# A hybrid encoder layer on one core: the memory attention in two lanes, longer steps for the power, and the w_down sums in the places of x

## The chip, the cores and the metric

The kernel runs on one core of a Trainium2 chip. Its time is the time of one execution on the device, in microseconds (us); several executions of the same program give a median and a range. The profile is of one execution. PE is the TensorE matmul, PEld its weight load, DVE the VectorE, ACT the ScalarE, POOL the GpSimd engine and SP the engine whose queue issues every DMA of this kernel.

## The reference

One layer over 2048 tokens of 1024 channels, all in f32. After an RMS norm a large projection feeds three mixers; their outputs are gated, merged and projected back, and an MLP follows.

```
h = rmsnorm(x, g_mix);  z = h @ w_in
q_na = rmsnorm(q_na, g_na_q) * 32**-0.5;  k_na = rmsnorm(k_na, g_na_k)
h_na  = neighbourhood_attention(q_na, k_na, v_na, rpb)     # 8 heads of 32, window 8 x 16 of a 32 x 64 grid
h_m   = mlstm(...) forwards + backwards                    # 4 heads, 64 / 128
q = rmsnorm(q_mem) * 64**-0.5;  k = rmsnorm(k_mem)         # 4 heads of 64
h_mem = softmax(q @ k.T) @ v                               # into 256 memory tokens
y = gate0 * (h_m @ w_proj_mlstm) + gate1 * (h_na @ w_proj_na) + gate2 * (h_mem @ w_proj_mem)
x = x + y @ w_out
x = x + square(relu(rmsnorm(x, g_ffn) @ w_up)) @ w_down
```

## The kernel before

Each f32 product is made of three matmuls on a high and a low part (`mm3`, L232 to L234). Weights come in units of 512 KB: a load (L172), the high part by ACT (L176) and the low part by DVE (L177). The large MLP products are replaced by seven of quarter size instead of eight, for which sums of blocks of w_down are made ahead (`sums_down`).

There are three phases. **Phase 1** takes the tokens in four blocks of 512. In a block come, in this order, the query and key columns of the neighbourhood attention (four groups of 24 matmuls, one for each tile of 128 tokens), the mLSTM's queries and keys with their convolution (`conv`: four groups, whose PSUM result ACT copies out at L654, and some seven DVE operations on each), the neighbourhood values with the memory queries (L519 to L530), the mLSTM's values, in blocks 2 and 3 the 24 groups of the gates (`gate`, copied out at L599), and the output gates. Phase 2 is the scan of the mLSTM with the remaining gates, phase 3 the merge, the output projection and the MLP.

The order of PE's work is the order in which the program is written. After every two steps of a group (six matmuls), now and then four, a **tick** happens: `tick` calls each of three streams once, and a stream gives one piece of small work to the engines. `self.tk` counts the ticks modulo 4.

- `na_qk` (one unit for each tile of tokens): squares by ACT (L917), their sums by DVE (L919), the reciprocal root by POOL with a power (`rstd`, L324 and L325), the product by DVE (L922), PE transposes (L927), high and low parts, stores to DRAM (`s_qs`, `s_ks`). A `yield` ends a piece.
- `mem_unit`, the same for the memory queries, followed by scores (L1184), maximum (L1187), exponential (L1191), transposes (L1204), copies (L1206, tile `mpT`) and the values (L1214).
- `na_stream`, the neighbourhood attention proper. A unit is four heads; queries and keys are loaded by six DMAs (L1008, L1009: `naq`, `nak`), the values by two (`nav`) and a table of biases for each head (`nab`, L1033). A head's scores are L1042, its bias and maximum L1045, its exponential L1047, its scaling L1050, its transposes L1061 five ticks later, and the values L1075. A head starts every four ticks, in block 3 every two.

`unit_stream(q, lanes)` has so many units under way as there are lanes; a lane names the values of `tk` at which its unit may step. Only PE's order is fixed by the program. For ACT, DVE, POOL and SP a scheduler takes operations in the order in which it expects them to be ready, with a priority that the kernel lowers or raises (`cur_priority`), so that an operation can stand on its engine well ahead of work that was written before it. Each of these engines then works strictly in its own order, SP with its waits too.

`sums_down` loads two units of w_down (tiles `dw`, L576), makes four differences in place on DVE at a low priority (L579), and stores both to `s_t` (L101). Eight of these belong to block 2 and eight to block 3, each at every third gate. `x_tile` gives the two buffers (`xt`, 512 KB each) through which tiles of x come in, `x_junk` a tile for squares of which only the sum is used.

## Time and profile before

| what | value |
|---|---|
| median of three runs | 2989.27 us (2983.28 to 2989.3) |
| profiled execution: its time | 2988.64 us |
| profiled execution: span from first to last instruction | 2986.9 us |
| mean granted clock of TensorE | 0.995 |
| PE busy | 2910.6 us (97%) |
| DVE / ACT / POOL busy | 2070.4 / 1195.1 / 237.1 us |
| HBM read / written | 453.63 MB / 176.55 MB |

A row of a list of waits names who waited, for whom, the total, the number of times and the longest. A row of a timeline has the start, the length, the engine, the line and the operation, and in brackets the idle time before it with what ended it. A row of windows has, for a stretch of time, each engine's busy time with its number of instructions, the granted clock, and the DMA's share and rate.

### The profile page before, as it was taken

Reading aid. Unit: us, or ns where it says so; the run is one execution under the profiler, and the core shown is the slowest. Engines: PE = TensorE matmul, PEld = TensorE weight load, DVE = VectorE, ACT = ScalarE, POOL = GpSimd, SP = SyncE. Lnnn points to the kernel's source line nnn. Section 1 sums busy time; section 2 is a strip of 40 time slices with the busy share of each in tenths; the row PEclk is TensorE's granted clock in tenths of the full one; section 3 lists DMA queues with packets and bytes.
Section 4 is the critical chain, followed back from the end, with each engine's and each line's share of the span. In section 5 each row is a group of like instructions: output and inputs, shape, how many; then the busy total and the mean of one; then the engine's idle time right before and its main releaser. Section 6 shows DMA issues by size and latency. Waiting matters only on the chain.

```text
span 2986.9 us, 41900 instructions
## 1 busy us (share of the span) xinstructions
PE 2910.6 (97%) x15028; PEld 2374.8 (80%) x15028; DVE 2070.4 (69%) x3557; ACT 1195.1 (40%) x2198; POOL 237.1 (8%) x389
## 2 busy tenths in 40 slices
PE   8999999999999899999999999999999999999999
PEld 6778788878877677778888888888878888888887
DVE  6676775567654765674769888666676888885666
ACT  6454654344543333342233333543312433344331
POOL 3020210011000322330000000000000000000000
PEclk9999999999999999999999999999999999999999
DMA  8776777867799667789535444766874444466655
GB/s 276 225 253 202 231 227 240 266 217 217 240 283 307 195 199 234 240 276 315 183 110 169 155 152 155 275 191 224 268 235 128 137 155 151 154 226 225 195 182 165
DMA packets 341712, 632.97 MB, mean 212 GB/s; under 512 B 29344, under 2 KB 151008, under 8 KB 341504
## 3 DMA queue, kind: packets, MB, share of 16 engines
q1 hardware_dynamic: 341504, 630.30, 65.4%
q8 instruction: 118, 1.93, 0.3%
q14 instruction: 90, 0.74, 0.1%
HBM read 453.63 MB, written 176.55 MB: 211 GB/s over the span
## 4 chain that ended last, share of the span: by engine, by line
PE 55%; DVE 2%; DMA 2%; issue 1%; ACT 0%; POOL 0%; SPq 0%; DVEq 0%; ACTq 0%; POOLq 0%
PE mm L232 18%; PE mm L234 18%; PE mm L233 18%; PE mm L1339 0%; DVE h L900 0%; DMA og<-s_o 0%; DMA wr<-in_w_units_dram 0%; DMA hf<-s_hf 0%; DVE ev L1495 0%; ACT hf L896 0%; POOL rs L325 0%; DVE acc L1488 0%; DVE ws L177 0%; DVE h L888 0%; DMA X<-s_a 0%
## 5 line engine op out<-in xcount | busy, mean ns | idle before, releaser
L232 PE MATMUL mm<-X,ws 128*128 128x512 f32 x1152 | 448.5, 389 | 0.0
L234 PE MATMUL mm<-X,ws 128*128 128x512 f32 x1152 | 448.2, 389 | 0.0
L233 PE MATMUL mm<-X,ws 128*128 128x512 f32 x1152 | 448.1, 389 | 0.0
L232 PE MATMUL mm<-hT,ws 128*128 128x512 f32 x896 | 375.6, 419 | 12.1 <-ACT cz L654 5.5
L177 DVE TENSOR_TENSOR ws<-wr,ws 128x1024 fp32r<-128x1024 f32 (+1 forms) x212 | 263.0, 1246 | 142.8 <-ACT ws L176 137.7
L234 PE MATMUL mm<-hT,ws 128*128 128x512 f32 x896 | 353.6, 395 | 0.0
L233 PE MATMUL mm<-hT,ws 128*128 128x512 f32 x896 | 353.4, 394 | 0.0
L233 PE MATMUL mm<-X 128*128 128x512 f32 x896 | 348.8, 389 | 2.5 <-DVE X L1462 2.5
L234 PE MATMUL mm<-X 128*128 128x512 f32 x896 | 348.7, 389 | 0.5 <-DVE X L1462 0.5
L232 PE MATMUL mm<-X 128*128 128x512 f32 x896 | 348.7, 389 | 0.4 <-ACT X L1461 0.4
L1461 ACT ACTIVATE X<-X 128x1024 fp32r<-128x1024 f32 x176 | 187.0, 1063 | 319.4 <-DMA X<-s_t 124.5
L1462 DVE TENSOR_TENSOR X<-X 128x1024 fp32r<-128x1024 f32 x176 | 214.3, 1224 | 132.8 <-ACT X L1461 132.0
L176 ACT ACTIVATE ws<-wr 128x1024 fp32r<-128x1024 f32 (+1 forms) x212 | 223.5, 1059 | 164.7 <-PE mm L234 91.8
L232 PE MATMUL mm<-ws,hT 128*128 128x512 f32 (+2 forms) x704 | 260.9, 371 | 9.3 <-ACT cz L654 5.1
L234 PEld LDWEIGHTS mm<-X,ws 128*128 128x128 f32 x1152 | 216.2, 188 | 45.1
L233 PEld LDWEIGHTS mm<-X,ws 128*128 128x128 f32 x1152 | 216.2, 188 | 44.9
L232 PEld LDWEIGHTS mm<-X,ws 128*128 128x128 f32 x1152 | 216.2, 188 | 44.5
L234 PE MATMUL mm<-ws,hT 128*128 128x512 f32 (+2 forms) x704 | 249.8, 355 | 1.1 <-DVE hT L434 1.1
L233 PE MATMUL mm<-ws,hT 128*128 128x512 f32 (+2 forms) x704 | 249.0, 354 | 0.3 <-DVE ws L177 0.3
L202 ACT ACTIVATE ws<-wr 128x512 fp32r<-128x512 f32 x224 | 135.3, 630 | 219.9 <-PE mm L234 139.3
L232 PEld LDWEIGHTS mm<-hT,ws 128*128 128x128 f32 x896 | 170.2, 190 | 54.1 <-issue 9.8
L234 PEld LDWEIGHTS mm<-hT,ws 128*128 128x128 f32 x896 | 169.6, 189 | 39.0
(266 smaller groups left out, 4855.3 us busy)
## 6 DMA issues: line engine op xcount, KB each, us to landing
wr<-in_w_units_dram SPq DMA_DIRECT2D x308, 512.0 KB
s_s<-u SPq DMA_DIRECT2D x32, 1024.0 KB
X<-s_s SPq DMA_DIRECT2D x64, 512.0 KB
X<-s_t SPq DMA_DIRECT2D x64, 512.0 KB
s_g<-ev SPq DMA_DIRECT2D x96, 256.0 KB
ev<-s_g SPq DMA_DIRECT2D x96, 256.0 KB
s_a<-u SPq DMA_DIRECT2D x96, 256.0 KB
X<-s_a SPq DMA_DIRECT2D x48, 512.0 KB
```

The source lines that it names most:

```text
L176: nc.scalar.activation(w[:, 0], raw, AF.Copy)
L177: nc.vector.tensor_tensor(w[:, 1], raw, w[:, 0].bitcast(F32), ALU.subtract)
L202: nc.scalar.activation(hi, src, AF.Copy)
L232: mm(out, lhs[0], rhs[0], start=first, stop=False)
L233: mm(out, lhs[0], rhs[1], start=False, stop=False)
L234: mm(out, lhs[1], rhs[0], start=False, stop=last)
L1461: nc.scalar.activation(hi, src, AF.Copy)
L1462: nc.vector.tensor_tensor(lo, src, hi.bitcast(F32), ALU.subtract)
```

## The change

Memory attention gets two lanes, each of which steps every four ticks, in place of one that steps every two; one `yield` fewer stands before the scores and one fewer before the transposes. The tiles `mq`, `me` and `mpT` are doubled. The queries and keys of the neighbourhood attention step every two ticks instead of every four, with five pauses instead of two: from the sums to the product were four ticks, now there are six; from the product to the transposes there are four as before. `zna` has four buffers instead of three. `sums_down` uses the two buffers of x and is split: the loads are given at one gate, the differences and stores at the next, so that the eight sums of a block take its first sixteen gates. The biases have three buffers instead of four, and a unit of the neighbourhood attention that starts while no other is under way waits eight ticks after its loads instead of four. The squares for a norm are written over their input.

```diff
-NAB = 4
+NAB = 3
...
-        self.prep(xt, gbc, xt, self.x_junk())
+        self.prep(xt, gbc, xt, self.t("ev", [128, D], EV[1], BF16))
...
-        self.streams = [self.unit_stream(self.qkq, [(1,)]), self.unit_stream(self.memq, [(0, 2)]), self.na_stream()]
+        self.streams = [self.unit_stream(self.qkq, [(1, 3)]), self.unit_stream(self.memq, [(0,), (2,)]), self.na_stream()]
...
-            z = self.t("zna", [128, 512], 3)
+            z = self.t("zna", [128, 512], 4)
...
         if b in GATES_1:
+            sums = None
             for j in range(24):
                 if j == 22 and b + 1 < NB:
                     self.prep_x()
                 self.gate(b, j)
-                if j % 3 == 0:
-                    self.sums_down(8 * GATES_1.index(b) + j // 3)
+                if j < 16:
+                    sums = sums or self.sums_down(8 * GATES_1.index(b) + j // 2)
+                    sums = next(sums, None) and sums
...
+        r = [self.x_tile(self.a["w_units"][self.down[half * FF // 256 + q][0]]) for half in range(2)]
+        yield True
         prio = self.tc.cur_priority
         self.tc.cur_priority = prio + LOW
-        r = [self.t("dw", [128, 1024], 2) for _ in range(2)]
-        for half in range(2):
-            nc.sync.dma_start(r[half], self.a["w_units"][self.down[half * FF // 256 + q][0]])
...
         r = self.rstd(ss, 32, "q")
         yield
+        yield
+        yield
         nc.vector.tensor_tensor(z, z, r.unsqueeze(2).to_broadcast([128, 16, 32]), ALU.mult)
+        yield
         yield
...
-                last = self.na_unit(*todo.pop(0), last)
+                last = self.na_unit(*todo.pop(0), last, 4 if cur else 8)
...
-        q = self.t("mq", [128, 2, 2, 128], 1, F32R)
+        q = self.t("mq", [128, 2, 2, 128], 2, F32R)
         self.mem_trans(z, q, self.gmqk[:, 0:1])
-        yield
         yield
...
-            e = self.t("me", [128, 2, 256], 2)
+            e = self.t("me", [128, 2, 256], 4)
...
         yield
         yield
-        yield
         ptp = []
...
-            pT = self.t("mpT", [128, 4, 128], 2)
+            pT = self.t("mpT", [128, 4, 128], 4)
```

The same instructions are issued as before, apart from their tiles' names; in phases 2 and 3 they stand on every engine in the same order. In phase 1 they move. Three places of it follow; line numbers are those of each kernel (a memory exponential is L1191 before and L1190 now, a reduction of `na_qk` L919 and L916, its product L922 and L921, a copy out of the convolution L654 and L651, a load through `x_tile` L461).

ACT, ahead of the first convolution group of block 1. Before:

```order
L944 ACTIVATE stk_312_2122<-tr_310_2110,gna_404 128x2x128
L1047 ACTIVATE nsb_319_2153,sm_321_2156<-nsb_319_2153,sm_320_2154 128x440
L1191 ACTIVATE me_337_2223,sm_336_2222<-mx_333_2206,sm_335_2220 128x256 x2
L176 ACTIVATE ws_324_2165<-wr_324_2164 128x2x528
L1047 ACTIVATE nsb_344_2246,sm_346_2249<-nsb_344_2246,sm_345_2247 128x440
L1191 ACTIVATE me_341_2232,sm_340_2231<-mx_334_2207,sm_339_2229 128x256 x2
L654 ACTIVATE cz_348_2255<-mm_325_2169 128x512
```

And with the change:

```order
L1047 ACTIVATE nsb_320_2172,sm_322_2175<-nsb_320_2172,sm_321_2173 128x320
L1064 ACTIVATE npt_330_2203<-tr_329_2199 120x384
L944 ACTIVATE stk_314_2143<-tr_312_2131,gna_404 128x2x128
L1215 ACTIVATE mho_333_2231<-mx_332_2222 128x256
L651 ACTIVATE cz_339_2252<-mm_326_2188 128x512
```

The exponentials of block 0's last memory unit stood between the queries and keys and the copy `cz`; now that unit's last operation (`mho`) comes before it.

DVE, the sums of squares of block 1's last tile of tokens and the product that needs POOL's power. Before:

```order
L919 TENSOR_REDUCE sm_395_2514<-sq_394_2512 128x16
L1050 TENSOR_SCALAR nsb_319_2153<-nsb_319_2153,sm_322_2158 128x320
L922 TENSOR_TENSOR zna_323_2162<-zna_323_2162,rs_396_2516 128x512
L1187 TENSOR_REDUCE sm_335_2220<-mx_333_2206 128x2
L1045 ISA nsb_344_2246,sm_345_2247<-mx_343_2244,nab0_1_0_3_1948 128x320
```

And with the change:

```order
L916 TENSOR_REDUCE sm_395_2610<-sq_394_2608 128x16
L945 SCALAR_TENSOR_TENSOR stk_314_2143<-tr_312_2131,gna_404,stk_314_2143 128x2x128
L1050 TENSOR_SCALAR nsb_320_2172<-nsb_320_2172,sm_323_2177 128x320
L921 TENSOR_TENSOR zna_324_2181<-zna_324_2181,rs_396_2612 128x512
L1216 TENSOR_TENSOR mho_333_2231<-mx_332_2222,mho_333_2231 128x256
L1045 ISA nsb_335_2243,sm_336_2244<-mx_334_2241,nab0_1_0_2_2034 128x320
```

One operation stood between sums and product, now two; the memory maximum (L1187) behind the product is gone from there.

SP's queue in block 3, from a bias of the unit of rows 6 to the loads of the unit of rows 7. Before:

```order
L1033 DMA nab6_1_1_3_9628<-in_rpb_dram 128x440
L1008 DMA naq7_0_9653<-s_qs_96 32x4x256
L1009 DMA nak7_0_9654<-s_ks_97 32x4x512
L101 DMA s_t5_191<-dw_1686_9479 128x2x512
L101 DMA s_t5_191<-dw_1687_9480 128x2x512
L1008 DMA naq7_0_9653<-s_qs_96 32x4x256
L1009 DMA nak7_0_9654<-s_ks_97 32x4x512
L1008 DMA naq7_0_9653<-s_qs_96 32x4x256
L1009 DMA nak7_0_9654<-s_ks_97 32x4x512
```

And with the change:

```order
L101 DMA s_t6_192<-xt_1648_9365 128x2x512
L101 DMA s_t6_192<-xt_1649_9367 128x2x512
L101 DMA s_hna_131<-nho_1552_8912 256x1x256
L461 DMA xt_1685_9543<-in_w_units_dram 128x1024
L461 DMA xt_1686_9545<-in_w_units_dram 128x1024
L101 DMA s_g3_95<-ev_1704_9637 128x512
L172 DMA wr_1705_9646<-in_w_units_dram 128x1024
L1033 DMA nab6_1_1_2_9665<-in_rpb_dram 128x440
L1008 DMA naq7_0_9690<-s_qs_96 32x4x256
L1009 DMA nak7_0_9691<-s_ks_97 32x4x512
L1008 DMA naq7_0_9690<-s_qs_96 32x4x256
L1009 DMA nak7_0_9691<-s_ks_97 32x4x512
```

The stores of a sum no longer divide the loads of queries and keys. The loads of the next sum (`xt`) now stand one DMA behind the stores of the last, in the same two buffers.

More of the change, by code (lines that the diff above doesn't have):

```diff
@@ L442, in rms_x @@
             xt = self.x_tile(self.a["x"][r0:r0 + 128])
-            nc.scalar.activation(self.x_junk(), xt, AF.Square, accum_out=ss[:, t:t + 1])
+            nc.scalar.activation(xt, xt, AF.Square, accum_out=ss[:, t:t + 1])
             yield
@@ L448, in rms_x @@
         self.rb = self.gbc[:, b % 2 * TB:(b % 2 + 1) * TB]
-        dg = self.t("zna", [128, 512], 3).rearrange("p (t c) -> p t c", t=4)
+        dg = self.t("zna", [128, 512], 4).rearrange("p (t c) -> p t c", t=4)
         nc.vector.tensor_tensor(dg, self.ident.unsqueeze(1).to_broadcast([128, 4, 128]),
@@ L462, in x_tile @@
         return xt
-    def x_junk(self):
-        self.n += 1
-        return self.p_x.tile([128, D], BF16, name=f"xq_{self.n}", tag="xq", bufs=1)
     def lhs_tok(self, hT, k, t):
@@ L1010, in na_load_qk, with na_unit @@
         return q, k
-    def na_unit(self, g, hg, half, before):
+    def na_unit(self, g, hg, half, before, wait):
         nc = self.nc
@@ L1016, in na_unit @@
         nr = 8 if g in (0, 7) else 11
-        u = dict(g=g, hg=hg, half=half, nk=nr * 40, pts=[], h=0, wait=4)
+        u = dict(g=g, hg=hg, half=half, nk=nr * 40, pts=[], h=0, wait=wait)
         u["qk"] = before["qk"] if half else self.na_load_qk(g, hg, kr0, nr)
@@ L1134, in mem_rms @@
         for t in range(2):
-            nc.scalar.activation(self.x_junk(), mt[:, t], AF.Square, accum_out=ss[:, t:t + 1])
+            nc.scalar.activation(mt[:, t], mt[:, t], AF.Square, accum_out=ss[:, t:t + 1])
         rm = self.rstd(ss, D, "m")
```

## The prediction

> **What bounds the kernel now.** I read the page's first part, then windows by phase, then PE's waits in phase 1, and last the timelines round the largest of them.
>
> ```profile
> span 2986.9 us, 41900 instructions
> PE 2910.6 (97%) x15028; PEld 2374.8 (80%) x15028; DVE 2070.4 (69%) x3557; ACT 1195.1 (40%) x2198; POOL 237.1 (8%) x389
> ```
>
> ```profile
> 0.00:969.00 969.00, 924.18 (x5803) 758.79 (x5803) 615.54 (x1390) 484.61 (x1016) 109.37 (x217) 0.99 0.78 245
> 969.00:1376.00 407.00, 385.19 (x2112) 292.67 (x2113) 266.73 (x524) 154.62 (x412) 127.69 (x172) 0.98 0.73 231
> 1376.00:2986.90 1610.90, 1601.24 (x7116) 1323.29 (x7114) 1188.13 (x1643) 555.85 (x771) 0.00 (x0) 1.00 0.56 187
> ```
>
> PE is the bound (first number after each stretch's length). The change takes no matmul away, and phases 2 and 3 keep their order on every engine, so what it can win lies in the first row: 969.00 less 924.18 is 44.8 us of PE idle, and what the clock lost behind it. PE's waits in that stretch:
>
> ```profile
> PE mm L232 <- ACT cz L654: 10.6, 5, 2.7
> PE mx L232 <- ACT ws L176: 7.5, 1, 7.5
> PE mx L1042 <- DMA nav<-s_vna: 5.4, 1, 5.4
> PE tr L1061 <- DVE nsb L1050: 4.7, 2, 2.6
> PE mm L232 <- ACT zif L528: 4.2, 4, 1.7
> PE mm L232 <- DMA hT<-s_hT: 4.0, 1, 4.0
> PE mx L1214 <- ACT mpT L1206: 2.1, 2, 1.3
> ```
>
> The 7.5 us are the first weights at the start and the 4.0 us the reload of hT at the end of the phase; the change touches neither. The other five rows make 27.0 us in 14 pieces. Some are followed by a stretch of lower clock (the number before the last two):
>
> ```profile
> 81.00:85.00 4.00, 4.00 (x16) 2.96 (x15) 3.90 (x5) 0.84 (x2) 0.00 (x0) 0.57 0.94 272
> ...
> 231.00:235.00 4.00, 4.00 (x16) 2.97 (x16) 3.55 (x9) 0.18 (x1) 0.00 (x0) 0.57 0.76 208
> ...
> 644.00:648.00 4.00, 3.94 (x13) 3.33 (x14) 2.41 (x8) 1.69 (x5) 0.13 (x1) 0.57 0.81 164
> ...
> 869.00:873.00 4.00, 3.80 (x12) 3.14 (x12) 1.05 (x4) 0.66 (x2) 0.00 (x0) 0.50 1.06 408
> ```
>
> That is 4.00 times 0.43, 1.7 us, at each of the first three and 2.0 us at the last: 7.1 us. The pool is 27.0 + 7.1 = 34.1 us, 1.1% of the time. The sum is made against the profiled execution's own 2988.64 us (0.6 below the median of the three runs).
>
> The Trainium skill, "TensorE: Matmul & The Clock Gate", section "What's actually happening", has the clock fall after an idle window of about 3.4 us. By that rule the first three stretches, each behind idle pieces below 2.8 us, would not exist and no clock would come back with them; the trace shows them, so the measurement decides.
>
> **The change part by part.** First the w_down sums. In block 3 SP's queue, and PE, read:
>
> ```profile
> 853.23 0.68 SPq L1009 DMA_DIRECT2D nak<-s_ks  x1
> 860.67 0.90 SPq L101 DMA_DIRECT2D s_t<-dw  x2
> 861.62 0.87 SPq L1008 DMA_DIRECT2D naq<-s_qs  x1
> ...
> 864.29 0.47 SPq L1009 DMA_DIRECT2D nak<-s_ks  x1
> ```
>
> ```profile
> 863.22 0.40 PE L233 MATMUL mm<-hT,ws 128*128 128x512 f32 x1
> 863.45 0.40 PE L234 MATMUL mm<-hT,ws 128*128 128x512 f32 x1
> 869.20 0.60 PE L1042 MATMUL mx<-nak,naq 96*128 96x320 f32 x1 [5.35 <-DMA nav<-s_vna]
> ```
>
> SP stood from 853.9 to 860.7 for the differences of a sum, with four of the six loads of the next unit behind it; PE waited 5.35 us and lost 2.0 us of clock. At the end of block 2 the same happened to a tile of x:
>
> ```profile
> 603.11 0.91 SPq L172 DMA_DIRECT2D wr<-in_w_units_dram  x2
> 615.93 2.19 SPq L101 DMA_DIRECT2D s_t<-dw  x2
> ```
>
> ```profile
> 637.86 0.65 PE L1061 MATMUL tr<-ident,nsb 128*120 128x128 f32 x4 [2.09 <-DVE nsb L1050]
> ...
> 644.05 0.81 PE L1061 MATMUL tr<-ident,nsb 128*120 128x128 f32 x4 [2.57 <-DVE nsb L1050]
> ```
>
> The late tile kept DVE behind until the first of these two waits, 2.09 us. Sums cost 5.35 + 2.0 + 2.09 = 9.4 us now. With the change all eight are done by the sixteenth gate, far from the tile of x, and the order shows queries and keys in one piece. But sixteen pairs of stores remain in the same queue, each waiting for low-priority work of DVE. Bounds: nothing to 9.4 us back; I take two thirds, **-6.3**.
>
> Next the time for the powers. Block 1, DVE, then ACT, then PE:
>
> ```profile
> 203.58 0.69 DVE L922 TENSOR_TENSOR zna<-zna,rs 128x512 f32<-128x512 f32 x1 [3.08 <-POOL rs L325]
> 204.19 0.69 DVE L1187 TENSOR_REDUCE sm<-mx 128x2 f32<-128x512 f32 x1
> ```
>
> ```profile
> 204.91 0.48 ACT L1191 ACTIVATE me<-mx,sm 128x256 f32<-128x256 f32 x1 [6.15 <-DVE sm L1187]
> ...
> 208.25 0.59 ACT L654 ACTIVATE cz<-mm 128x512 f32<-128x512 f32 x1
> ```
>
> ```profile
> 208.90 0.50 PE L232 MATMUL mm<-hT,ws 128*128 128x512 f32 x1 [2.50 <-ACT cz L654]
> ```
>
> ```profile
> 359.55 0.50 PE L232 MATMUL mm<-hT,ws 128*128 128x512 f32 x1 [1.63 <-ACT cz L654]
> ```
>
> DVE stands for POOL's power; the memory maximum is queued behind, ACT waits for that maximum, and the convolution's copy is queued behind ACT's exponentials. The longer steps hardly move this: pauses hold PE's transposes back, but the scheduler still puts the product two or three DVE operations behind the sums, as the order shows. So I keep the total of
>
> ```profile
> DVE zna L922 <- POOL rs L325: 42.4, 15, 3.3
> ...
> DVE nsb L1045 <- DMA nab<-in_rpb_dram: 5.8, 4, 1.8
> ```
>
> as it is. What does go is what stood behind: two lanes finish the last memory unit before the next block's convolution, so no maximum and no exponential lies between power and copy. The 2.50 and 1.63 us come back whole. The 2.57 us at 644 sit behind a power too, and no memory work was in it; with its clock it is 4.3 us, half of which I take for the shifted steps. Together -4.1 - 2.1 = **-6.2** (bounds 0 and 8.4).
>
> The fourth convolution group of block 1 is late because DVE is full; block 0's also:
>
> ```profile
> 230.59 0.39 PE L232 MATMUL mm<-ws,hT 128*128 128x272 f32 x1 [2.72 <-ACT cz L654]
> ```
>
> With the clock this is 4.4 us. A memory unit's maxima, scaling and output (three rows of a list by line) leave this stretch:
>
> ```profile
> L1194 DVE TENSOR_TENSOR me<-me,sm 128x512 f32<-128x512 f32 x32 | 21.9, 685 | 0.1
> L1187 DVE TENSOR_REDUCE sm<-mx 128x2 f32<-128x512 f32 x32 | 21.7, 678 | 0.1
> ...
> L1218 DVE TENSOR_TENSOR mho<-mx,mho 128x256 fp32r<-128x256 f32 x16 | 6.7, 421 | 14.3 <-ACT mho L1217 14.2
> ```
>
> Twice 685, twice 678 and 421 ns are 3.1 us of DVE, about the wait; as some of it falls ahead of the wait's cause I take half, **-2.2** (0 to 4.4). Block 0's two convolution waits (10.6 less 2.50, 1.63 and 2.72: 3.8, with clock 5.5) have no earlier memory unit to lose; the third tile's q/k work comes later, for which a quarter, **-1.4** (0 to 5.5).
>
> The values of a memory unit came two ticks behind the last transposes, now four: the 2.1 us for mpT go, **-2.1** (0 to 2.1). The zif waits (4.2 us, a copy behind DVE's backlog) ease a little: **-1.0** (0 to 4.2). Doubled tiles and squares written in place cost nothing: the operations are the same, and ACT has half its time free behind PE.
>
> Against it: a bias is asked for two ticks after its buffer's scores, so three buffers leave four ticks of lead at rate two where four left six. From the rows at 863 a matmul starts every 0.23 us; six make a tick of 1.4 us, so 5.6 us of lead instead of 8.4. DVE waited 5.8 us for biases in all; I let it wait that once more and PE pay it: **+5.8**. Its bounds are 0 and the 32 us of the slow case below. The eight ticks at a block's start delay the end of the stream by four ticks, 5.6 us; in the built order its last values still stand ahead of the last output gates on PE, so that no tick runs empty at the end.
>
> Sum: -6.3 - 6.2 - 2.2 - 1.4 - 2.1 - 1.0 + 5.8 = -13.4; 2988.64 - 13.4 = **2975.2 us**.
>
> **Rivals.** (B) The change doesn't do what it says: powers and convolution stall as before, only elsewhere. For it: the 42.4 us above and the order. Left are sums, mpT and biases: -6.3 - 2.1 + 5.8 = -2.6, 2986.0 us. (C) Every piece of the pool goes and the biases cost their 5.8: -28.3, 2960.3 us. For it: all pieces are short queues behind one another, which one loosening can end together; against it: the powers stay. (D) Slower, by SP's queue. The loads of a sum now wait for the last sum's stores to land, since they use the same two buffers. A transfer of 512 KB took
>
> ```profile
> 1241.81 3.62 DMA wr<-in_w_units_dram
> ```
>
> in the chain of waits, so SP stands some 3.6 us, with biases and weights behind, sixteen times. In block 3, where heads come every two ticks, a bias can then come after the 5.6 us of lead, DVE stands, and the transposes of that head are late as at 637 and 644: 4.7 / 2 = 2.3 us and 1.7 us of clock for each of eight sums, 32 us; -19.2 + 32 = +12.8, 3001.4 us. It decides from 19.2 / 8 = 2.4 us a sum. Against it: a store held SP for up to 12 us before (603 to 616) and only two pieces reached PE.
>
> The Trainium skill, "DMA: Bandwidth & Descriptors", section "Anatomy of one DMA", speaks against the change here: a wait is held by the issuing queue, and completion of a write to HBM takes about 2 us beside the bytes. An estimate by its fit is 2.0 + 1.2 = 3.2 us for a store of 512 KB, near the 3.62 us of the row; no row shows such a store's own landing.
>
> **How the numbers follow.** Forecast (A) 0.52, B 0.25, C 0.11, D 0.12. About 0.2%, 6 us, is what a measurement of this kernel can tell from no change. Below 2983.3 us lie nearly all of A (0.48), C (0.11) and a fifth of B (0.05): faster 0.64. Within: the rest of A (0.04), most of B (0.19) and an edge of D (0.02): 0.25. Slower: D and a little of B, 0.11. The range runs from C's value to just over B's, 2961 to 2988; some 0.05 lie below and 0.13 above.
>
> **What would show it.** In PE's waits of phase 1: cz at about 5 us (right), at 10 (B) or gone (C); the 5.4 us for a unit's loads gone, with SP's wait for s_t spread over more and shorter pieces; mpT gone; the L922 wait still near 42 us (if it is below 25, my reading of the steps was wrong and C is nearer). DVE's wait for biases above 12 us, or new waits of L1061 in block 3, speak for D. Phases 2 and 3 must last as long as before to within 3 us; if they differ by more, the sum was made over the wrong stretch.

## The result

The changed kernel takes **3005.66 us** (median of four runs, 3004.55 to 3008.78), the kernel before beside it 2989.28: a ratio of **1.0064, 95% interval 1.005 to 1.0078**. It is slower by 16.4 us in the medians and by some 19 by the ratio; 2975.2 us was forecast, in a range of 2961 to 2988. The profiled execution has a span of 3003.5 us (2986.9 before) and a mean granted clock of 0.989 (0.995).

PE's waits up to phase 2, answering to the list that the prediction shows:

```profile
PE tr L1061 <- DVE nsb L1050: 13.9, 4, 7.7
PE mx L1042 <- DMA nab<-in_rpb_dram: 13.2, 2, 6.6
PE mx L1042 <- DMA s_g<-ev: 8.4, 1, 8.4
PE mx L232 <- ACT ws L176: 7.2, 1, 7.2
PE mm L232 <- DMA hT<-s_hT: 4.0, 1, 4.0
PE mm L232 <- ACT cz L651: 3.9, 2, 3.5
PE mm L232 <- ACT zif L524: 1.1, 2, 0.6
```

What was to go went: the convolution's copy from 10.6 to 3.9 us, zif from 4.2 to 1.1, mpT altogether. But before the transposes of a head (L1061) and the first scores of an attention unit (L1042) PE now waits 35.5 us (13.9 + 13.2 + 8.4) instead of 10.1.

Where they lie shows when phase 1 is cut at the copies of the gates on ACT (L599 before, L596 after): up to block 2's first gate, its 24 gates, the way to block 3's first gate, its 24 gates, to phase 2's first gate, the rest. The second number of a row is the length, the third PE's busy time, the number before the last two the clock, the next the DMA's share. Before:

```profile
0.00:444.60 444.60, 418.31 (x2595) 346.62 (x2596) 308.13 (x700) 244.92 (x515) 79.82 (x114) 0.99 0.75 235
444.60:602.10 157.50, 157.50 (x961) 127.93 (x960) 80.98 (x169) 67.36 (x137) 3.21 (x23) 1.00 0.83 257
602.10:759.90 157.80, 149.97 (x957) 124.51 (x959) 110.47 (x250) 78.52 (x167) 20.85 (x40) 0.99 0.69 214
759.90:943.20 183.30, 176.66 (x1202) 142.01 (x1202) 108.79 (x265) 86.00 (x188) 5.48 (x40) 0.98 0.88 278
982.40:2986.90 2004.50, 1973.04 (x9183) 1605.51 (x9181) 1442.32 (x2144) 708.39 (x1179) 118.75 (x154) 1.00 0.60 196
```

After:

```profile
0.00:427.70 427.70, 413.41 (x2598) 346.33 (x2599) 303.64 (x679) 246.06 (x514) 76.11 (x113) 1.00 0.75 238
427.70:583.30 155.60, 155.60 (x927) 126.20 (x929) 85.92 (x181) 65.93 (x133) 3.18 (x23) 1.00 0.85 274
583.30:752.40 169.10, 154.30 (x998) 129.48 (x991) 109.15 (x251) 81.69 (x172) 21.28 (x39) 0.96 0.65 199
752.40:957.30 204.90, 181.06 (x1179) 144.16 (x1181) 114.49 (x276) 85.08 (x189) 5.85 (x42) 0.93 0.84 259
997.50:3003.50 2006.00, 1974.73 (x9182) 1607.81 (x9180) 1443.87 (x2144) 708.13 (x1179) 118.99 (x154) 1.00 0.60 196
```

The changed kernel is 16.9 us ahead at block 2's first gate and 18.8 at its last. It loses 11.3 us on the way to block 3 and 21.6 us in block 3's gates; with +1.0 to phase 2 and +1.5 behind, the difference of the spans, 16.6 us, is complete. In block 3's gates 23.8 us are idle (204.90 less 181.06). PE is also busy there 8.8 us longer than in the same gates of e9 below, where it never waits (172.30): the mean clock of the stage is 0.93 here and 1.00 there.

Two more lists, DVE's waits and SP's, of the changed kernel:

```profile
DVE zna L921 <- POOL rs L325: 40.4, 16, 4.3
DVE nsb L1045 <- DMA nab<-in_rpb_dram: 27.8, 14, 5.9
```

```profile
SPq L461 <- DMA s_t<-xt: 43.6, 21, 4.9
```

The wait for POOL's power is what it was (42.4), that for biases five times as long (5.8), and SP stands 43.6 us for the landing of the sums' stores. One piece of block 3, SP's queue, then PE:

```profile
814.02 1.03 SPq L101 DMA_DIRECT2D s_t<-xt  x2
815.15 1.16 SPq L1033 DMA_DIRECT2D nab<-in_rpb_dram  x1
819.13 1.62 SPq L461 DMA_DIRECT2D xt<-in_w_units_dram  x2
...
824.29 0.73 SPq L1008 DMA_DIRECT2D naq<-s_qs  x1
...
828.29 0.43 SPq L1009 DMA_DIRECT2D nak<-s_ks  x1
```

```profile
837.47 0.70 PE L1042 MATMUL mx<-nak,naq 96*128 96x440 f32 x1 [6.63 <-DMA nab<-in_rpb_dram]
```

The loads of a sum stand some 4 us behind its predecessor's stores, the unit's queries and keys behind them, and its first scores come 8.7 us after the last of these loads was given. My first theory (**S**) was that SP's wait for the landing makes the unit late. Rivals: **N**, three bias buffers are too few; **L**, the longer steps put the units later; and, from e7 on, **T**, the traffic of sixteen dense gates.

### The profile page after: what moved, and what is told of

Read it like the earlier page. It is cut to its first block, busy times and chain, and to the rows that moved or that the text cites. A ratio compares the mean times of both kernels' runs of the same rounds, so it can differ in the third digit from the quotient of the medians.

```text
span 3003.5 us, 41885 instructions
## 1 busy us (share of the span) xinstructions
PE 2915.3 (97%) x15028; PEld 2383.0 (79%) x15028; DVE 2074.8 (69%) x3557; ACT 1196.9 (40%) x2198; POOL 234.4 (8%) x389
## 2 busy tenths in 40 slices
DMA packets 341712, 632.97 MB, mean 211 GB/s; under 512 B 29344, under 2 KB 151008, under 8 KB 341504
## 4 chain that ended last, share of the span: by engine, by line
PE 55%; DVE 2%; DMA 1%; issue 0%; ACT 0%; SPq 0%; POOL 0%; DVEq 0%; ACTq 0%; POOLq 0%
PE mm L232 18%; PE mm L234 18%; PE mm L233 18%; DMA hf<-s_hf 1%; PE mm L1337 0%; DMA wr<-in_w_units_dram 0%; PE pn L859 0%; DVE h L897 0%; PE pn L862 0%; DVE ev L1493 0%; DVE acc L1486 0%; ACT hf L893 0%; POOL rs L325 0%; DMA X<-s_a 0%; DVE ws L177 0%
## 5 line engine op out<-in xcount | busy, mean ns | idle before, releaser
L176 ACT ACTIVATE ws<-wr 128x1024 fp32r<-128x1024 f32 (+1 forms) x212 | 223.3, 1058 | 158.1 <-PE mm L234 86.6
```

What stands on the lines that cost most here:

```text
L176: nc.scalar.activation(w[:, 0], raw, AF.Copy)
```

## The experiments

All times below are medians; each ratio is against the kernel before on the same chip (2985.2 to 2988.3 us there). The stages are those of the rows above, read from one profiled execution of each. What lies behind them took 2004.1 to 2010.5 us in these executions, though nothing was changed there, so a few us of a single reading can be chance. e1, e2, e9, e10 and e18 leave out the differences of some or all sums: they are probes, not kernels to use.

| kernel | us | ratio, 95% interval | to block 2 | its gates | way to block 3 | its gates | to phase 2 |
|---|---|---|---|---|---|---|---|
| before | 2989.28 | | 444.6 | 157.5 | 157.8 | 183.3 | 39.2 |
| the change | 3005.66 | 1.0064 (1.005, 1.0078) | 427.7 | 155.6 | 169.1 | 204.9 | 40.2 |
| e1 sums copied | 2964.48 | 0.993 (0.9914, 0.9946) | 431.8 | 156.4 | 153.3 | 172.3 | 39.0 |
| e2 before, sums copied | 2970.39 | 0.9952 (0.9935, 0.9968) | 447.7 | 157.5 | 149.0 | 174.3 | 38.2 |
| e3 four biases | 3012.22 | 1.0091 (1.0074, 1.0108) | 429.5 | 158.0 | 171.8 | 202.5 | 39.8 |
| e4 every third gate | 2985.21 | 1.0003 (0.9993, 1.0012) | 429.5 | 156.5 | 169.1 | 183.2 | 40.0 |
| e5 sums back | 2986.18 | 0.9994 (0.9983, 1.0004) | 433.2 | 156.6 | 165.0 | 182.3 | 40.2 |
| e6 sums alone | 3016.34 | 1.0099 (1.0085, 1.0114) | 442.6 | 161.6 | 161.2 | 203.5 | 39.3 |
| e7 GpSimd's queue | 3027.67 | 1.0129 (1.0115, 1.0143) | 454.6 | 165.9 | 182.1 | 176.1 | 39.2 |
| e8 three gates | 2985.90 | 0.9993 (0.9984, 1.0003) | 428.4 | 156.5 | 169.0 | 181.7 | 40.8 |
| e9 copied in block 3 | 2974.23 | 0.9955 (0.9941, 0.9969) | 431.0 | 159.4 | 166.3 | 172.3 | 40.3 |
| e10 copied in block 2 | 2991.11 | 1.0012 (1.0002, 1.0021) | 430.2 | 156.5 | 152.0 | 203.7 | 39.3 |
| e11 blocks 1 and 2 | 3005.43 | 1.0059 (1.0047, 1.0072) | 442.2 | 170.2 | 174.9 | 172.4 | 40.0 |
| e12 spread | 2981.56 | 0.9984 (0.9974, 0.9994) | 428.7 | 156.4 | 152.1 | 189.7 | 47.0 |
| e13 spread, four biases | 2980.56 | 0.9983 (0.9974, 0.9992) | 430.3 | 156.5 | 149.9 | 189.9 | 47.5 |
| e14 spread, old steps | 2988.90 | 1.0 (0.9992, 1.0009) | 430.6 | 156.4 | 153.6 | 192.9 | 48.1 |
| e15 six and ten | 2988.75 | 1.0011 (1.0001, 1.002) | 428.4 | 156.5 | 158.1 | 191.7 | 42.8 |
| e16 seven and nine | 2986.46 | 1.0 (0.9991, 1.001) | 429.0 | 156.7 | 161.3 | 190.6 | 41.3 |
| e17 two pairs | 2992.07 | 1.0018 (1.0009, 1.0027) | 434.6 | 156.5 | 156.3 | 195.3 | 40.2 |
| e18 copied, dense | 2987.18 | 1.0006 (0.9995, 1.0017) | 430.8 | 156.5 | 158.0 | 195.4 | 40.0 |

### What the sums cost, and in whose company

In e1, and likewise in e2 for the sums of the kernel before:

```diff
-                if j < 16:
-                    sums = sums or self.sums_down(8 * GATES_1.index(b) + j // 2)
-                    sums = next(sums, None) and sums
+                if j % 3 == 0:
+                    q = 8 * GATES_1.index(b) + j // 3
+                    for half in range(2):
+                        self.store(self.scr["t"][q // 2][:, half, :, q % 2],
+                                   self.a["w_units"][self.down[half * FF // 256 + q][0]].rearrange("p (n c) -> p n c", n=2))
```

> The changed kernel without its w_down sums: at every third gate the two weight halves are copied from memory to memory into the place of the sums, by transfers that wait for nothing (the differences are left out, so the output is not the reference's). Theory S (SP is held by the sums' loads, which wait until the stores of the sum before have landed in the same two buffers, and the loads of the next attention unit stand behind): the 6.63, 6.61 and 8.37 us ahead of a unit's first scores go, most of the 2.76, 4.35 and 7.69 us at the end of block 2 as well, 37.7 us in all less what stays of them, and the time is 2962 to 2978 us. Theory N (three bias buffers are too few; 14 waits of VectorE for biases, 27.8 us): the waits stay, and the time is above 2995. Theory L (longer steps put the attention units later): also above 2995.

> The kernel before without its sums, copied in the same way at the same gates (differences left out). It prices what the sums cost the kernel before: I put 9.4 us on them, so 2980 us; beside the run of the changed kernel without sums it gives what the other parts of the change are worth where no sum disturbs them: my sum has 13.0 us less 5.8 for the biases.

With copies in place of the sums the changed kernel takes 2964.48 us, in S's range and far from N's and L's. The kernel before takes 2970.39: there the sums cost 14.8 us more than such copies, not my 9.4. So the other parts of the change are worth 5.9 us where no sum disturbs them (the prediction's terms for them: 12.9 less 5.8, 7.1). In the profiled executions they win 15.9 us up to block 2's first gate, and 4.3 of these are lost again on the way to block 3 (153.3 against 149.0).

One thing about these probes matters below. A copy waits for nothing, so the scheduler did not leave it at its gate: the first is given at 89 us, and of the sixteen that e1 writes behind block 3's gates one is given during them. The copies given during these gates (their number, the ns that an issue took, the first and the last time), in e1 and in e18, a later probe with twice as many:

```profile
L101 SPq DMA_DIRECT2D s_t<-in_w_units_dram x1: 598/598/598, 892.4 to 892.4; - x1
```

```profile
L101 SPq DMA_DIRECT2D s_t<-in_w_units_dram x29: 537/594/1162, 748.4 to 883.7; - x29
```

So e1's 172.3 us are block 3's gates all but free of the sums' transfers (e2 gives five copies there, e9 three), not gates with sparse copies.

In e3:

```diff
-NAB = 3
+NAB = 4
...
-            pT = self.t("mpT", [128, 4, 128], 4)
+            pT = self.t("mpT", [128, 4, 128], 3)
```

> The changed kernel with four bias buffers instead of three (one buffer less for mpT, 3 instead of 4, makes the room). Theory S: VectorE's 27.8 us for biases fall a little, the three waits ahead of a unit's first scores stay above 5 us each, and the time is 2999 to 3007. Theory N: waits and new stalls go, 2972 to 2990.

DVE's waits for biases fall from 27.8 to 17.2 us, and the kernel gets no faster: 3012.22 us, 5 above S's range, with waits of 7.4 to 8.5 us at three units' first scores and one of 12.0 for which the profile names no releaser. N falls.

In e6, on the kernel before (`sums_down` is that of the change):

```diff
-                if j % 3 == 0:
-                    self.sums_down(8 * GATES_1.index(b) + j // 3)
+                if j < 16:
+                    sums = sums or self.sums_down(8 * GATES_1.index(b) + j // 2)
+                    sums = next(sums, None) and sums
...
-        r = [self.t("dw", [128, 1024], 2) for _ in range(2)]
+        r = [self.x_tile(self.a["w_units"][self.down[half * FF // 256 + q][0]]) for half in range(2)]
+        yield True
...
```

> The kernel before with the change of the sums alone: in the places of x, loads at the even gates, the rest at the odd ones, done by the sixteenth. In the changed kernel the sums cost 44.8 us of phase 1 (984.04 against 939.26 without them), in the kernel before 15.8. If that is the sums' own doing, this kernel loses 29 us, 3010 to 3018 us, with PE's waits at the first scores of a unit. If it takes the other parts of the change, 2983 to 2998.

The piece on sums alone makes the kernel before 0.99% slower, 28 us; L falls too. It is the sums' own doing, and all other parts together then win back about a third of a per cent (1.0064 against 1.0099).

### Spacing, other buffers, another queue

In e4, and then in e8, where `sums_down` has a second `yield` ahead of its stores and block 3's first tile of x is fetched behind the last gate:

```diff
-                if j < 16:
-                    sums = sums or self.sums_down(8 * GATES_1.index(b) + j // 2)
-                    sums = next(sums, None) and sums
+                if j % 3 == 0:
+                    for _ in self.sums_down(8 * GATES_1.index(b) + j // 3):
+                        pass
```

```diff
-                if j < 16:
-                    sums = sums or self.sums_down(8 * GATES_1.index(b) + j // 2)
-                    sums = next(sums, None) and sums
+                sums = self.sums_down(8 * GATES_1.index(b) + j // 3) if j % 3 == 0 else sums
+                next(sums, None)
```

> The changed kernel with each sum in one piece at every third gate, as before, in the places of x as now. The stores of the sum before are then three gates old when the next loads are given. Theory S: SP's 43.6 us for the landing of s_t go to below 15 and the time is 2972 to 2990. Theory N and theory L: no sign of the sums' spacing, 3000 to 3008.

> The changed kernel with a sum over three gates: loads behind the first, differences behind the second, stores behind the third (the tile of x that was fetched at gate 22 is fetched behind the last gate). Theory S: the stores are given when the differences are long done, and the next loads when the stores were given one gate before; SyncE's waits for s_t and for the differences fall below 15 us, 2966 to 2982. Rival: the order that the scheduler gives the queue decides and not the gates, then as with every third gate, 2983 to 2990.

Block 3's gates fall to 183.2 and 181.7 us, and SP's wait for the landing to 8.1 and 9.4 us: S's figures. During these gates SP gives 29 and 30 of the sums' transfers, as many as in the change (30), only further apart. But the way between the blocks stays at 169 in both, and e8 misses S's range by it and lies in its rival's.

In e5 (the loads at a low priority, as before), and then in e7:

```diff
-                if j < 16:
-                    sums = sums or self.sums_down(8 * GATES_1.index(b) + j // 2)
-                    sums = next(sums, None) and sums
+                if j % 3 == 0:
+                    self.sums_down(8 * GATES_1.index(b) + j // 3)
...
-        r = [self.x_tile(self.a["w_units"][self.down[half * FF // 256 + q][0]]) for half in range(2)]
-        yield True
+        r = [self.t("dw", [128, 1024], 2) for _ in range(2)]
...
-            e = self.t("me", [128, 2, 256], 4)
+            e = self.t("me", [128, 2, 256], 2)
...
-            pT = self.t("mpT", [128, 4, 128], 4)
+            pT = self.t("mpT", [128, 4, 128], 2)
```

```diff
-    def x_tile(self, src):
+    def x_tile(self, src, queue=None):
...
-        self.nc.sync.dma_start(xt, src)
+        (queue or self.nc.sync).dma_start(xt, src)
...
-        r = [self.x_tile(self.a["w_units"][self.down[half * FF // 256 + q][0]]) for half in range(2)]
+        r = [self.x_tile(self.a["w_units"][self.down[half * FF // 256 + q][0]], nc.gpsimd) for half in range(2)]
...
-            self.store(self.scr["t"][q // 2][:, half, :, q % 2], r[half].rearrange("p (n c) -> p n c", n=2))
+            nc.gpsimd.dma_start(self.scr["t"][q // 2][:, half, :, q % 2], r[half].rearrange("p (n c) -> p n c", n=2))
```

> The changed kernel with the sums as they were: own buffers, every third gate, loads of low priority (me and mpT go back to two buffers each to make the room). So it has all parts of the change but the sums. If the sums alone made the change slow, and cost here what they cost the kernel before (2985.2 less 2970.4 without them, 14.8 us), the time is 2964.5 + 14.8, 2979 us. If the other parts bring the sums out of step (three bias buffers, the attention units later), it is 2985 or more.

> The changed kernel with the loads and stores of the sums on GpSimd's queue instead of SyncE's; their number, sizes, gates and buffers stay. Theory S (it is SyncE standing for the landing of stores that makes the units' loads late): the waits of 6.6 to 8.4 us at a unit's first scores go and the time is 2966 to 2985; GpSimd's powers may be held instead, which VectorE's 40.4 us wait at L921 would show. Rival T (the traffic or VectorE's work of sixteen dense gates): no better than 2998.

e5 is no better than the kernel before, which is its second branch: 11.4 us ahead at block 2, it loses 7.2 on the way between the blocks, so with the old sums too the rest of the change costs something there. e7 missed S's range; it meets T's condition, but does not answer its question: on GpSimd's queue the scheduler started the sums at 318 us, blocks ahead of their gates, and GpSimd stood 66.6 us for landings and 58.5 us for differences, with the powers behind in its order. Block 3's gates, with sums in their first 20 us only, took 176.1 us.

### Which block's sums

In e9; e10 has 2 and 3 exchanged:

```diff
-                if j < 16:
+                if b == 2 and j < 16:
                     sums = sums or self.sums_down(8 * GATES_1.index(b) + j // 2)
                     sums = next(sums, None) and sums
+                if b == 3 and j % 3 == 0:
+                    q = 8 * GATES_1.index(b) + j // 3
+                    for half in range(2):
+                        self.store(self.scr["t"][q // 2][:, half, :, q % 2],
+                                   self.a["w_units"][self.down[half * FF // 256 + q][0]].rearrange("p (n c) -> p n c", n=2))
```

> The changed kernel with its eight sums in block 2 as they are, and those of block 3 replaced by copies from memory to memory at every third gate (eight sums are left out). Theory S3 (sums cost where attention runs two heads to a period, block 3, and nothing in block 2): the gates of block 3 fall from 204.9 to about 172 us, as with all sums copied; the way from the last gate of block 2 to the first of block 3 tells whether its 169.1 us (153.3 with all sums copied) belong to the sums of block 2 (stays 165 to 170, time 2969 to 2975) or to the first sum of block 3 (falls to 153 to 157, time 2956 to 2962).

> The other half: block 2's eight sums copied, block 3's as in the changed kernel. Theory S3: the gates of block 3 stay at 200 to 206 us. The way between the blocks then answers the other way round: 153 to 157 if the sums of block 2 had lengthened it (time 2988 to 2994), 165 to 170 if the first sum of block 3 had (3001 to 3006).

The two halves nearly add up: over e1, these two stages together take 13.0 us more in e9, 30.1 in e10 and 48.4 in the change. Block 3's sums cost 31 us in block 3's gates (203.7 against 172.3). Block 2's cost 14 us on the way to block 3, where none of their stores is given any more. The two rows of each kernel, the way and block 3's gates, first with sums in block 2 alone, then in block 3 alone:

```profile
590.40:756.70 166.30, 151.20 (x961) 127.02 (x960) 108.91 (x250) 80.40 (x171) 20.05 (x39) 0.96 0.65 199
756.70:929.00 172.30, 172.30 (x1176) 138.81 (x1177) 95.23 (x244) 85.07 (x189) 6.13 (x42) 1.00 0.74 222
```

```profile
586.70:738.70 152.00, 149.63 (x966) 126.28 (x967) 108.78 (x246) 79.55 (x171) 21.82 (x39) 0.99 0.68 206
738.70:942.40 203.70, 181.45 (x1176) 144.59 (x1177) 112.31 (x272) 85.81 (x189) 5.89 (x42) 0.93 0.84 258
```

In e11 `sums_step` takes the next of a sum's two steps; it is called behind the na/memory groups of block 1, behind two value groups of block 1 and all of block 2, and at block 2's gates:

```diff
+            if b == 1:
+                self.sums_step()
...
+            if b == 2 or b == 1 and t < PREP_V:
+                self.sums_step()
...
-                if j < 16:
-                    sums = sums or self.sums_down(8 * GATES_1.index(b) + j // 2)
-                    sums = next(sums, None) and sums
+                if b == 2 and j < 22:
+                    self.sums_step()
```

> The changed kernel with all sixteen sums (nothing left out) ahead of block 3: two behind the na/memory groups and one behind the value groups of block 1, two behind the value groups of block 2 and eleven at its first 22 gates, each over two steps as now. Theory S3: block 3's gates take 172 to 176 us instead of 204.9, and the time is 2968 to 2978, below both kernels. Rival: the sums' waits on SyncE cost the same in blocks 1 and 2, then the stages there grow by some 2 us a sum and the time is 2985 or more.

Block 3's gates took 172.4 us as expected, and the rest of the expectation was wrong: the first stages grew by 14.5 us, block 2's gates by 14.6, and the way to block 3 by 5.8. So sums also cost where attention runs at half the rate, as the rival had it; only block 2's gates had taken eight at every second gate without growing. Whether the wait or the traffic costs it there was not separated (SP waits 50.2 us for landings in e11).

### The way to block 3: what SP's order has to do with it

In the change SP's queue, and DVE, read between the blocks:

```profile
591.25 0.33 SPq L461 DMA_DIRECT2D xt<-in_xT_dram  x1
591.87 0.33 SPq L1033 DMA_DIRECT2D nab<-in_rpb_dram  x1
606.85 0.33 SPq L172 DMA_DIRECT2D wr<-in_w_units_dram  x1
607.22 0.43 SPq L101 DMA_DIRECT2D s_o<-ev  x1
607.69 0.43 SPq L461 DMA_DIRECT2D xt<-in_xT_dram  x1
608.17 0.50 SPq L1033 DMA_DIRECT2D nab<-in_rpb_dram  x1
```

```profile
604.94 0.69 DVE L1066 COPY npt<-tr 120x512 f32<-120x512 f32 x1 [4.22 <-PE tr L1061]
605.59 1.23 DVE L177 TENSOR_TENSOR ws<-wr,ws 128x1024 fp32r<-128x1024 f32 x1
```

For 14.6 us SP gives nothing: a weight load waits for its buffer, which DVE frees at 606.8, and the output's store, a tile of x and a bias stand behind. PE's waits on this way, 14.8 us in all, come after it, the last so much later that the rows do not tie it to this stand:

```profile
613.20 0.50 PE L232 MATMUL mm<-ws,hT 128*128 128x512 f32 x1 [2.76 <-ACT ev L554]
619.22 1.08 PE L1061 MATMUL tr<-ident,nsb 128*120 128x128 f32 x4 [4.35 <-DVE nsb L1050]
...
658.32 1.08 PE L1061 MATMUL tr<-ident,nsb 128*120 128x128 f32 x4 [7.68 <-DVE nsb L1050]
```

The kernel with copies in block 2 (e10) has the same piece in another order, the weight load last:

```profile
593.96 0.33 SPq L101 DMA_DIRECT2D s_o<-ev  x1
594.59 0.33 SPq L461 DMA_DIRECT2D xt<-in_xT_dram  x1
594.97 0.44 SPq L1038 DMA_DIRECT2D nab<-in_rpb_dram  x1
...
610.25 2.12 SPq L172 DMA_DIRECT2D wr<-in_w_units_dram  x2
```

Through the kernels the way goes with that order. With this weight load (the 93rd of the kernel) ahead of block 2's first output store it took 166 to 175 us (the change, e3, e4, e8, e9, e11). It is not all, though. In the kernel before, in e5 and in e6 the load stands behind that store, but SP stands 8 to 14 us ahead of the store all the same, for a sum's stores or for the weight load before: 157.8, 165.0 and 161.2 us. And e7, with the load behind the store, took 182.1 us with its sums on GpSimd's queue. The next kernels were chosen for another order:

In e12, with `sums_step` behind the first four value groups and the first two output groups of block 3 as well; e13 adds the edit of e3, e14 takes the queries' and keys' lane and pauses back to `[(1,)]` and two:

```diff
-                if j < 16:
-                    sums = sums or self.sums_down(8 * GATES_1.index(b) + j // 2)
-                    sums = next(sums, None) and sums
+                st, n = (4, 5) if b == 2 else (3, 8)
+                if j < st * n and j % st < 2:
+                    self.sums_step()
```

In e15; e16 has (0, 3, 6, 9, 12, 15, 18) and (0, 3, 6, 8, 11, 14, 16, 19, 22):

```diff
-                if j < 16:
-                    sums = sums or self.sums_down(8 * GATES_1.index(b) + j // 2)
+                if j in ((0, 3, 6, 9, 12, 15) if b == 2 else (0, 2, 5, 7, 10, 12, 15, 17, 20, 22)):
+                    sums = self.sums_down((6 + 0 if b == 3 else 0) + ((0, 3, 6, 9, 12, 15) if b == 2 else (0, 2, 5, 7, 10, 12, 15, 17, 20, 22)).index(j))
+                    next(sums)
+                elif sums:
                     sums = next(sums, None) and sums
```

> The changed kernel with the sixteen sums spread wide (nothing left out): five in block 2, at every fourth gate, two behind the value groups of block 3, eight at every third of its gates, one behind its output groups; each over two steps as now. In the built order of SyncE the loads of the first weights of block 3 then stand behind the output stores, the tile of x and the bias, as in the kernels whose way from block 2's gates to block 3's was 149 to 158 us, and not ahead of them as in those with 165 to 175. Theory O (that order makes the way long, not a sum that still runs): 150 to 156 us there. Block 3's gates as with every third gate, 180 to 184. Together 427.7 + 156 + 153 + 182 + 40 + 2006 = 2965 us, and 3 to 6 us for the three sums outside gates: 2964 to 2974, below both kernels. Rival: the sums lengthen that way whatever the order: 165 or more there and 2980 or more in all.

> The spread sums with four bias buffers instead of three (three for mpT instead of four). My prediction put +5.8 us on the third buffer: then this is 4 to 8 us faster than the run with three. If the biases wait because of what SyncE stands for and not because of their number, the two are within 3 us.

> The spread sums with the queries' and keys' steps as before: one step a period and the pauses as they were. My prediction gave the waits at the convolution to the memory lanes more than to these steps (the powers stay, since the scheduler sets the products, not the pauses): the first gate of block 2 then comes within 5 us of the run with the new steps. If the new steps are what frees the convolution, it comes 8 to 17 us later and PE's wait for cz goes back to 8 us or more.

> The changed kernel with six sums in block 2 (every third gate from the first) and ten in block 3 (its gates 0, 2, 5, 7, 10, 12, 15, 17, 20, 22), each over two gates, nothing left out. In SyncE's order no weight load stands ahead of the first three output stores of block 2. Theory O: the way between the blocks 150 to 158 us. Block 3's gates: ten sums at 1.2 to 2.2 us over 172.3, so 184 to 194; no sum behind the output groups, so 40 us to phase 2 instead of 47.0. In all 428 + 156 + 154 + 189 + 40 + 2006 = 2973 us, 2966 to 2980. Rival: 165 or more between the blocks, 2985 and more.

> Seven sums in block 2 (every third gate) and nine in block 3 (gates 0, 3, 6, 8, 11, 14, 16, 19, 22). Here SyncE's order has one weight load ahead of the second output store of block 2, not of the first as in the changed kernel, and one bias ahead of the next weight load at the convolution. Theory O: between the two groups, 155 to 166 us on the way between the blocks; block 3's gates 182 to 192; 2973 to 2990 in all.

The way came out as the order said: 152.1 (e12), 149.9, 153.6, 158.1 (e15, 0.1 us over its range), and 161.3 for the mixed order (e16). That the order lengthens the way is borne out by these forecasts, though not shown alone: no run changed nothing but the order, and why the scheduler turns it round when more sums stand in block 2 stays open.

The totals of e12 and e15 missed; e16's is in its range. e12 and e13 are the best that compute everything, at 2981.56 and 2980.56 us, **0.9984 and 0.9983 of the kernel before (0.9974 to 0.9994 and 0.9974 to 0.9992)**. But in e12 block 3's gates took 189.7 us instead of 182, and the way to phase 2 47.0 us instead of 40 (42.8 and 41.3 in e15 and e16, which have no sum written behind the output groups). With ten sums in block 3 (e15) nothing is left of the gain.

The pair e12 and e13 answers for the biases: three buffers or four (with one fewer for mpT) make no difference to the time (0.9984 and 0.9983), though DVE waits 16.6 us for biases with three and 10.0 with four. e14 shows that the gain ahead of block 2 came with the memory lanes and their tiles, since with the old query and key steps its first gate still comes at 430.6 us and cz waits 3.0; the new steps themselves are worth some 5 us by the ratios and 7 by the medians (2988.90 less 2981.56), in small pieces of several stages; the two intervals just overlap.

### The wait or the traffic

Spacing had changed two things at once. The last two kernels keep the traffic and take the wait away.

In e17 (me and mpT with two buffers, as in e5), and then in e18:

```diff
-        r = [self.x_tile(self.a["w_units"][self.down[half * FF // 256 + q][0]]) for half in range(2)]
+        src = [self.a["w_units"][self.down[half * FF // 256 + q][0]] for half in range(2)]
+        if q % 2:
+            r = [self.t("dw", [128, 1024], 2) for _ in range(2)]
+            for half in range(2):
+                nc.sync.dma_start(r[half], src[half])
+        else:
+            r = [self.x_tile(s) for s in src]
```

```diff
                 if j < 16:
-                    sums = sums or self.sums_down(8 * GATES_1.index(b) + j // 2)
-                    sums = next(sums, None) and sums
+                    for half in range(2):
+                        self.store(self.scr["t"][j // 2][:, half, :, j % 2],
+                                   self.a["w_units"][self.down[half * FF // 256 + j][0]].rearrange("p (n c) -> p n c", n=2))
```

> The changed kernel with the same sums at the same sixteen gates, in turn in the places of x and in a pair of buffers of their own (me and mpT with two buffers make the room), so that the stores of a pair are four gates old when its next loads are given. Traffic, cadence and differences stay; only SyncE's wait for the landing goes. Theory S (the wait): block 3's gates 174 to 186 us instead of 204.9. Theory T (the traffic of sixteen dense gates delays the units' loads): 195 to 206. SyncE's order between the blocks is that of the good group but for one weight load: 150 to 160 us there. With S 2966 to 2984 us in all, with T 2988 to 3000.

> The changed kernel with copies instead of sums again (differences left out), but as many transfers as the sums make, at the same gates: two copies of 512 KB from memory to memory behind each of the sixteen gates, none with a wait. Theory S: block 3's gates as with the sparse copies, 172 to 177 us; theory T: 190 or more.

Both read T's number: 195.3 and 195.4 us in block 3's gates, with 31 transfers of sums given during them in e17 and 29 copies in e18. In e17 SP's waits for s_t are down to a few of at most 1.7 us; in e18 there is no sum at all, so neither a landing to wait for nor a difference for DVE. Of the 32.6 us that the sums cost there (204.9 less 172.3), **23 come with the traffic** and 9.6 are the rest, the wait for the landing among it. S held only for that smaller part. With e4 and e8 the 23 divide once more: the same number of transfers spread over 24 gates costs some 10 us (181.7 and 183.2 against 172.3), and that they stand closer together the other 13.

Two limits. The order of SP's queue moved in e17 and e18 as well. And a copy reads and writes HBM in one transfer: e18 moves as many DMA bytes as the change (632.96 and 632.97 MB), but 16.8 MB more are read and 16.8 MB more written in HBM. That the two kernels meet in one number is partly chance.

The window from 815 to 845 us, first in the change, then in e1, then with dense copies (e18), and last in the kernel before:

```profile
815.00:845.00 30.00, 23.37 (x138) 18.38 (x137) 15.93 (x37) 11.01 (x24) 0.67 (x5) 0.83 1.03 312
```

```profile
815.00:845.00 30.00, 30.00 (x202) 24.38 (x203) 16.48 (x42) 14.79 (x31) 1.28 (x8) 1.00 0.76 229
```

```profile
815.00:845.00 30.00, 24.90 (x166) 19.24 (x166) 13.46 (x37) 12.21 (x26) 0.80 (x6) 0.94 0.91 288
```

```profile
815.00:845.00 30.00, 28.71 (x207) 23.02 (x206) 19.72 (x49) 16.13 (x38) 0.93 (x7) 1.00 0.98 285
```

At a DMA share of 0.76 PE never waits here; at 0.91 and 1.03 it loses 5 and 7 us of 30, but at 0.98, in the kernel before, only 1.3. Over the whole stage the share is even lower in the change (0.84) than before (0.88), and block 2's gates of the change have 0.85 with PE always busy. So a high share goes with the loss but does not measure it. The scores at 837.47 fit a late landing, since the unit's loads had been given 8.7 us earlier; but no row has a landing, and the load that PE's row names is that of a bias, which these scores do not read. How the dense transfers make PE wait therefore stays an inference.

## Why the prediction was wrong

**The bound** was read rightly: everything that changed lies in phase 1, and phases 2 and 3 differ by 1.5 us, inside the 3 us that were allowed.

**The sums, -6.3, is the step that failed.** Its bounds were "nothing to 9.4 us back", which left no room for a loss. The sums' piece alone costs 28 us on the kernel before (e6). In block 3's gates, where it costs 32.6 us over gates without sums, the runs show dense transfers (23) and what goes with the wait for the landing (9.6) in place of the relief. Three things were missed. The sums cost the kernel before 14.8 us more than early copies (e2), not 9.4: their visible waits were not all of their price. "All eight are done by the sixteenth gate" was counted as relief for the tile of x, and not as half as much traffic again for each gate. And of the row at 869, quoted for its clock, I did not read the share of DMA, 1.06 at 408 GB/s, a hint that transfers stood close in block 3 already.

**Powers and convolution, -12.9 in five terms** (6.2, 2.2, 1.4, 2.1, 1.0), was right in mechanism ahead of block 2 and not far off in size: 16.9 us were won up to block 2's first gate, 12.8 to 16.2 in e1, e3, e4, e8, e9, e10 and e12, which have the same steps and lanes and other sums or biases behind. It was not the whole account: e1 against e2 has 5.9 us left of it in the medians and 11.3 in the profiled spans (2973.0 less 2961.7), with 4.3 lost on the way to block 3. The waits went as told: cz 10.6 to 3.9, zif 4.2 to 1.1, mpT gone, L921 still at 40.4. One part was wrong: half of the wait at 644 was to go, and its successor at block 3's start became 7.7 us. That the doubled tiles "cost nothing" hid that they may be part of the gain: with two buffers for me and mpT block 2 begins at 433.2 and 434.6 us (e5 and e17), against 427.7 to 431.8 in the kernels above; there too some sums are given earlier.

**The biases, +5.8**, were nothing in the time: e12 and e13 are equal. DVE's waits for biases do fall with a fourth buffer (27.8 to 17.2 us in e3), but the time does not follow them: e5 has 35.9 us of them and takes as long as the kernel before.

**Rival D** (slower, by SP's queue, 3001.4 us, chance 0.12) had the sign and, by luck, nearly the time, but mostly not the reason. Its signals came: 27.8 us of DVE waits for biases, new waits of L1061. Its mechanism, the landing of stores, is within the 9.6 us of block 3's gates; 23 come with the traffic, and some 14 more are the way between the blocks (e9 against e10), where the built order of SP had the weight load ahead of the store. Against D stood that a store had held SP for up to 12 us before and only two pieces had reached PE; e2 prices those sums 5 us higher. On the landing itself D took 3.62 us. The Trainium skill, "DMA: Bandwidth & Descriptors", section "Anatomy of one DMA", led to an estimate of 3.2; that fit is for a single DMA issued by GpSimd, these are issued by SP. The trace has 4.1 us from the end of the stores' issue (815.05) to the load that waited (819.13), and up to 4.9 us of standing. That the wait is held by the issuing queue, as this section says, the trace bears out: SP's 43.6 us for s_t, with the DMAs of its queue behind.

**Chances.** 0.11 for slower was too little because the loss was kept out of the term and put into a rival whose price was then fought with an average. Had the sums' bounds reached from -9.4 to D's +32, the middle would have been a loss.

## What to carry to other kernels

Transfers that are moved closer together can cost as much as the waits that one sees: here some 13 us in one stage for the same number of them. Count the transfers for each step of the work before counting waits; the DMA's share is a warning, not a price. Buffers that are reused at once turn a store's landing into a wait of the queue, and everything later in this queue waits too; but take the wait away with the traffic kept before calling it the cause. When a probe replaces work by something that waits for nothing, look in the queue where it was given: here most of e1's copies were given long before their gates. A change whose parts are good and bad is worth splitting: one run of each part would have shown here that the lanes win and that the sums lose more.

## What was not expected of the hardware

29 copies of 512 KB from memory to memory, none behind a wait of its own, made block 3's gates 23 us longer (e18) than one or three (172.30 us with PE busy 172.30 us in e9), at only 266 GB/s over the stage and a DMA share of 0.84. Neither the share nor the rate tells a stage that suffers from one that does not: block 2's gates of the change took 0.85 at 274 GB/s, with 25 of the sums' transfers given during them and heads at half block 3's rate, without any idle time of PE.

After an idle time of 6.6 us the clock stayed low for some 8 us; in the change, behind the wait at 837.47:

```profile
837.47:841.47 4.00, 4.00 (x12) 3.27 (x13) 1.86 (x6) 0.75 (x2) 0.00 (x0) 0.50 1.04 410
841.47:845.47 4.00, 4.00 (x15) 3.13 (x15) 1.39 (x2) 2.78 (x5) 0.13 (x1) 0.74 0.87 271
```

Four microseconds at 0.50 and four at 0.74 are 3.0 us of lost clock on 6.6 us of waiting.
